# Low part of every fourth down-projection weight piece from a negated ScalarE copy and an accumulating transfer, in a one-core decoder layer

## The chip, the cores and the metric

The kernel runs on one core of a Trainium2 chip. The metric is the device time of one execution in microseconds (us); it is given as the median of several runs.

## What is computed

One decoder layer on 256 tokens of width 2048, in float32. The part that the change touches is the last matrix product, the down-projection of the gated MLP, followed by a residual and a layer norm:

```python
def conv_ffn(x, w_up, conv_w, conv_b, w_down):
    h = x @ w_up                                  # (256, 2048) @ (2048, 11264)
    ...                                           # causal depthwise conv, width 3
    a, b = jnp.split(acc, 2, axis=-1)
    return (jax.nn.silu(a) * b) @ w_down          # (256, 5632) @ (5632, 2048)

x = layer_norm(DN_ALPHA * x + conv_ffn(x, ...), ln2_g, ln2_b)
```

## The kernel before

TensorE multiplies in a float32 format of reduced precision (fp32r). To keep float32 accuracy every operand is split into a high part, which is the value rounded to fp32r, and a low part, which is the value minus the high part; a product is then the sum of three matmuls: high by high, high by low, low by high.

The down-projection is computed in four column blocks of 512 outputs (lines 907 to 917, the last block in a call of its own). Each block is one call of `tok_major`: the weights are the moving operand, the activations `aT` (already split) the stationary one. The 44 contraction tiles of 128 rows are brought in by `pieces` (line 81): one 1 MiB transfer on SP's queue (line 87) loads four tiles into a buffer `raw`, of which there are two (`RAW_BUFS = 2`); the buffer is then split in two pieces of two tiles, 128 x 1024 values each. So a block has 11 raw loads and 22 pieces. For a piece, `split` (line 72) lets ScalarE write the high part `whi` (an `act` copy with rounding, recorded at line 70) and VectorE the low part `wlo` (a subtraction, line 74). `whi` and `wlo` have four buffers each, so a piece's split can begin when TensorE is done with the piece four earlier. TensorE runs 12 matmuls of 512 columns on a piece (lines 149 to 151: per tile and token half one with `whi`, one with `wlo`, one with `whi` again).

A raw buffer is loaded anew when both of its pieces have been split, that is when the last reader of it is done; the loads are issued by SP in order. TensorE's order is written out by hand. The other engines' order in this stage is the scheduler's, with the split of the pieces at high priority in program order. GpSimd (POOL) does nothing for the weights here: at the start of the stage its queue issues two 1 MiB loads of the layer norm's rows (lines 911 and 912), at the end it takes part in the layer norm.

Of the kernel before, what the change touches and what calls it, by code (L numbers as in the profile page):

```python
# [11 lines left out]
AF = mybir.ActivationFunctionType  # L12
ALU = mybir.AluOpType
# [11 lines left out]
KF = DFF // P  # L25
# [16 lines left out]
def hybrid_layer(  # L42
# [6 lines left out]
    nc = tc.nc  # L49
    ctx.enter_context(tc.manual_schedule(engines={ENG.PE}))  # L50
    x2 = x[0]
    win, wup, wout, wdown = w_in[0], w_up[0], w_out[0], w_down[0]

    def hp(level=1):
        return tc.high_priority(offset=1000000 * level)
# [10 lines left out]
    def stt(o, a, s, b, op0, op1):  # L66
        nc.vector.scalar_tensor_tensor(out=o, in0=a, scalar=s, in1=b, op0=op0, op1=op1)  # L67

    def act(o, a, f, **kw):
        nc.scalar.activation(out=o, in_=a, func=f, **kw)  # L70

    def split(hi, lo, src, low=nc.vector):
        act(hi, src, AF.Copy)
        low.tensor_tensor(out=lo, in0=src, in1=hi.bitcast(F32), op=ALU.subtract)  # L74
# [6 lines left out]
    def pieces(w2, col, width, kt_n, big, step, home=None, low=lambda k0: nc.vector):  # L81
        wv = w2.rearrange("(k p) c -> p k c", p=P)
        for b0 in range(0, kt_n, big):
            bn = min(big, kt_n - b0)
            with hp():
                raw = wst.tile([P, bn, width], F32, name="raw", bufs=RAW_BUFS)
                nc.sync.dma_start(out=raw, in_=wv[:, b0:b0 + bn, col:col + width])
            for s0 in range(0, bn, step):
                n = min(step, bn - s0)
                with hp():  # L90
                    hi, lo = (home or stage)(b0 + s0, n, width)
                    split(hi, lo, raw[:, s0:s0 + n, :], low(b0 + s0))
                yield b0 + s0, n, hi, lo

    def stage(k0, n, width):
# [2 lines left out]
    def mm_tile():  # L98
        return ps_mm.tile([P, 2, 512], F32, name="mm")
# [14 lines left out]
    def feat_major(w2, col, xT, kt_n, big=8, step=4, ready=()):  # L114
        ps = mm_tile()
        for piece in ready or pieces(w2, col, 256, kt_n, big, step):
            fm_piece(ps, xT, kt_n, *piece)
        return ps
# [16 lines left out]
                                         stop=kt == kt_n - 1)  # L135
        return ps

    def tok_major(w2, col, xT, kt_n, big=4, step=2, last=0, home=None, done=None, during={}, ends=(512,), mid={}):
        if last:
            ps = [mm_tile()[:, 0, :] for _ in range(NT)]  # L140
        else:
            both = mm_tile()
            ps = [both[:, t, :] for t in range(NT)]

        def go(kt, t, hi, lo, k, o=None, w=slice(0, 512), first=0):
            o = ps[t] if o is None else o
            xs = slice(t * P, (t + 1) * P)
            xl = slice(S + t * P, S + (t + 1) * P)
            nc.tensor.matmul(o[:, w], lhsT=xT(kt)[:, xs], rhs=hi[:, k, w], start=kt == first, stop=False)  # L149
            nc.tensor.matmul(o[:, w], lhsT=xT(kt)[:, xs], rhs=lo[:, k, w], start=False, stop=False)  # L150
            nc.tensor.matmul(o[:, w], lhsT=xT(kt)[:, xl], rhs=hi[:, k, w], start=False, stop=kt == kt_n - 1)  # L151

        kept = []
        for k0, n, hi, lo in pieces(w2, col, 512, kt_n, big, step, home=home):
            if k0 < kt_n - last:
                for k in range(n):
                    for t in range(NT):
                        go(k0 + k, t, hi, lo, k)
                    for f in mid.get(k0 + k, ()):
                        f()  # L160
            else:
                kept.append((k0, n, hi, lo))
                for k in range(n):
                    go(k0 + k, 0, hi, lo, k)
        if last:
            done(0, ps[0], 0, 512)
        c0 = 0
        for c1 in ends if last else ():
            left = last
            o = mm_tile()[:, 0, :] if c0 else ps[1]  # L170
            for k0, n, hi, lo in kept:
                for k in range(n):
                    go(k0 + k, 1, hi, lo, k, o, slice(c0, c1), kept[0][0] if c0 else 0)
                    left -= 1
                    for f in during.get(left, ()):
                        f()
            done(1, o, c0, c1)
            c0 = c1
        return ps
# [47 lines left out]
    def xT(k):  # L227
        return xT_t[:, k, :]
# [72 lines left out]
    pooled = []  # L301

    second = pieces(win, 4096 + 256, 256, KD, 8, 4)
    early = []

# [67 lines left out]
    for j in range(2):  # L373
        ps = tok_major(win, 6144 + 512 * j, xT, KD)
        with hp():
            for t in range(NT):
                act(vg[t][:, 512 * j:512 * (j + 1)], ps[t], AF.Gelu_apprx_tanh)
# [10 lines left out]
    for j in range(4):  # L388
        crow = lv()[0:88, 0:P]
        src = conv_w[0, j] if j < 3 else conv_b[0]  # L390
# [36 lines left out]
    for j in range(4):  # L427
        ps = feat_major(win, 5120 + 256 * j, xT, KD)
# [10 lines left out]
    def hgrn(half):  # L439
        h0 = 4 * half  # L440
        fr, q, v, og = t4(), t4(), t4(), t4()
        for j in range(2):
            ps = feat_major(win, 1024 + 512 * half + 256 * j, xT, KD)
            fm_sum(bc(fr, S)[:, 2 * j:2 * j + 2, :], ps, mix)
        for j in range(2):
            ps = feat_major(win, 512 * half + 256 * j, xT, KD)
            qj = bc(q, S)[:, 2 * j:2 * j + 2, :]
            fm_sum(qj, ps, mix)
            with hp():
                act(qj, qj, AF.Silu)  # L450
        v = v.rearrange("p (t c) -> p t c", t=NT)
        ps = tok_major(win, 2048 + 512 * half, xT, KD)
        with hp():
            for t in range(NT):
                act(v[:, t, :], ps[t], AF.Copy)
        for j in range(2):
            ps = feat_major(win, 3072 + 512 * half + 256 * j, xT, KD)
            oj = bc(og, S)[:, 2 * j:2 * j + 2, :]
            fm_sum(oj, ps, mix)
            with hp():  # L460
                act(oj, oj, AF.Silu)

        return fr, q, v, og
# [153 lines left out]
    def open_gate(gi, j, home, mid={}):  # L617
        ps = tok_major(win, 7168 + D * gi + 512 * j, xT, KD, mid=mid)
        with hp():
            for t in range(NT):  # L620
                act(home[t], ps[t], AF.Sigmoid)
# [125 lines left out]
    for j in range(3):  # L747
        cs = slice(512 * j, 512 * (j + 1))
        ps = tok_major(wout, 512 * j, mT, KD) if j else first_out
# [34 lines left out]
    def wout_during(c):  # L784
        with hp(2):
            ln1_turn(0, c)
            if 0 < c < 3:
                ln1_low(0, c - 1)
            if c == 2:
                pull()  # L790

    tok_major(wout, 1536, mT, KD, last=KEEP, home=keep_home, done=wout_done,
              during={left: [lambda c=c: wout_during(c)] for c, left in enumerate((5, 3, 2, 0))})
# [32 lines left out]
    for j in range(KF // 2):  # L826
        ac = []
        for half in range(2):
            if j == 0 and half == 0:
                ps = ps_first  # L830
            else:
                ps = feat_major(wup, half * DFF + 256 * j, x1T, KD, ready=() if j else chain(up_early, up_next))
# [73 lines left out]

    for j in range(3):
        cs = slice(512 * j, 512 * (j + 1))
        ps = tok_major(wdown, 512 * j, aT, KF)
        if j == 0:  # L910
            nc.gpsimd.dma_start(out=g2[:, 0, :], in_=ln2_g[0].partition_broadcast(P))
            nc.gpsimd.dma_start(out=g2[:, 1, :], in_=ln2_b[0].partition_broadcast(P))
        with hp():
            for t in range(NT):
                stt(x1[:, t, cs], x1[:, t, cs], ALPHA, ps[t], ALU.mult, ALU.add)
                nc.vector.bn_stats(out=st2[:, t, j, :], in_=x1[:, t, cs])
# [43 lines left out]
```

## Time and profile before

| | us |
|---|---|
| median of three runs | 1600.36 |
| their range | 1599.52 to 1601.9 |
| the profiled execution's own time | 1600.03 |
| its span, first to last instruction | 1598.3 |

The profiled execution took 1.7 us more than its span, which lies outside the first and last instruction. Its mean granted TensorE clock was 0.997 of full speed. TensorE is the busiest engine by far; the rows below show how far ahead of it the other engines and the transfers are in the down-projection, which runs from about 1347 us to about 1587 us of the span.

### The profile page before, as it was taken

What the parts mean: (1) busy time and instruction counts of PE and PEld (TensorE: products, weight loads), DVE (VectorE), ACT (ScalarE), POOL (GpSimd) and SP (SyncE); (2) the same over time, 40 slices, a digit from 0 to 9 for tenths busy, and PEclk for the clock granted to TensorE, in tenths of its full rate; (3) what the DMA queues carried; (4) which work ended last, traced back from release to release, by engine and by line L of the source; (5) the groups of instructions that cost most, each with busy time, mean ns of one, the idle gap of its engine ahead of it and who ended that gap; (6) DMA issues with size and microseconds to landing.
All of it is one profiled execution on the core that took longest, in us unless ns stands there. A gap on an engine that the chain in (4) does not pass through costs nothing. (4 is left out here: it accounts for less than half of the span.)

```text
span 1598.3 us, 20294 instructions
## 1 busy us (share of the span) xinstructions
PE 1578.2 (99%) x8129; PEld 1344.8 (84%) x8129; DVE 1001.7 (63%) x1196; ACT 828.8 (52%) x962; POOL 48.4 (3%) x116
## 2 busy tenths in 40 slices
PE   9999999999999999999999999999999999999997
PEld 7888888888888887888888888888888888888886
DVE  6666547765448755447567677676676667445455
ACT  5455558546458555444435555555555555333332
POOL 1100000000000001000003000000000000000001
PEclk9999999999999999999999999999999999999999
DMA  7656555655555547655553655555655556655553
GB/s 246 234 185 198 185 191 174 195 178 169 192 189 172 199 160 263 211 186 183 187 208 106 210 186 184 186 191 194 193 184 185 187 192 231 208 185 201 193 186 130
DMA packets 217213, 305.10 MB, mean 191 GB/s; under 512 B 5148, under 2 KB 137812, under 8 KB 216608
## 3 DMA queue, kind: packets, MB, share of 16 engines
q1 hardware_dynamic: 214912, 294.67, 55.8%
q0 software_dynamic: 2208, 9.16, 1.7%
q8 instruction: 63, 1.03, 0.3%
q14 instruction: 30, 0.25, 0.0%
HBM read 301.71 MB, written 2.10 MB: 190 GB/s over the span
## 5 line engine op out<-in xcount | busy, mean ns | idle before, releaser
L74 DVE TENSOR_TENSOR wlo<-raw,whi 128x1024 fp32r<-128x1024 f32 x541 | 659.1, 1222 | 530.4 <-ACT whi L70 529.7
L70 ACT ACTIVATE whi<-raw 128x1024 fp32r<-128x1024 f32 x543 | 571.1, 1056 | 664.2 <-PE mm L151 281.6
L108 PE MATMUL mm<-x1T,whi 128*128 128x512 f32 x1376 | 432.2, 395 | 0.0
L111 PEld LDWEIGHTS mm<-x1T,wlo 128*128 128x128 f32 x1376 | 258.5, 188 | 61.1
L111 PE MATMUL mm<-x1T,wlo 128*128 128x256 f32 x1376 | 270.3, 278 | 0.0
L150 PE MATMUL mm<-wlo,X 128*128 128x512 f32 x612 | 238.4, 389 | 1.3 <-DVE wlo L74 1.3
L149 PE MATMUL mm<-whi,X 128*128 128x512 f32 x612 | 239.5, 391 | 0.0
L151 PE MATMUL mm<-whi,X 128*128 128x512 f32 x612 | 238.2, 389 | 0.0
L108 PEld LDWEIGHTS mm<-x1T,whi 128*128 128x128 f32 x1376 | 209.4, 189 | 0.0
L108 PE MATMUL mm<-X,whi 128*128 128x512 f32 x640 | 201.5, 396 | 0.9 <-DVE X L74 0.9
L111 PEld LDWEIGHTS mm<-X,wlo 128*128 128x128 f32 x640 | 120.2, 188 | 28.4
L150 PEld LDWEIGHTS mm<-wlo,X 128*128 128x128 f32 x612 | 114.9, 188 | 25.1 <-DVE wlo L74 2.0
L149 PE MATMUL mm<-whi,aT 128*128 128x512 f32 (+1 forms) x352 | 135.2, 384 | 0.0
L150 PE MATMUL mm<-wlo,aT 128*128 128x512 f32 (+1 forms) x352 | 135.2, 384 | 0.0
L151 PE MATMUL mm<-whi,aT 128*128 128x512 f32 (+1 forms) x352 | 135.2, 384 | 0.0
L151 PEld LDWEIGHTS mm<-whi,X 128*128 128x128 f32 x612 | 114.9, 188 | 24.1
L149 PEld LDWEIGHTS mm<-whi,X 128*128 128x128 f32 x612 | 114.9, 188 | 23.5 <-ACT whi L70 0.2
L111 PE MATMUL mm<-X,wlo 128*128 128x256 f32 x640 | 125.8, 278 | 0.0
L108 PEld LDWEIGHTS mm<-X,whi 128*128 128x128 f32 x640 | 97.7, 189 | 1.5 <-DVE X L74 1.2
L150 PEld LDWEIGHTS mm<-wlo,aT 128*128 128x128 f32 x352 | 66.1, 188 | 13.2
L151 PEld LDWEIGHTS mm<-whi,aT 128*128 128x128 f32 x352 | 66.1, 188 | 13.1
L149 PEld LDWEIGHTS mm<-whi,aT 128*128 128x128 f32 x352 | 66.1, 188 | 13.0
(189 smaller groups left out, 1281.1 us busy)
## 6 DMA issues: line engine op xcount, KB each, us to landing
raw<-in_w_in_dram SPq DMA_DIRECT2D x102, 1024.0 KB, 5.0
raw<-in_w_up_dram SPq DMA_DIRECT2D x88, 1024.0 KB, 5.1
raw<-in_w_down_dram SPq DMA_DIRECT2D x44, 1024.0 KB, 5.0
raw<-in_w_out_dram SPq DMA_DIRECT2D x16, 1024.0 KB, 5.1
raw<-in_w_pool_proj_dram SPq DMA_DIRECT2D x8, 1024.0 KB, 5.0
raw<-in_w_sg_proj_dram SPq DMA_DIRECT2D x8, 1024.0 KB, 5.1
raw<-in_w_hg_proj_dram SPq DMA_DIRECT2D x8, 1024.0 KB, 5.0
x<-in_x_dram POOLq DMA_DIRECT2D x4, 512.0 KB, 7.6
```

The source lines that it names most:

```text
L70: nc.scalar.activation(out=o, in_=a, func=f, **kw)
L74: low.tensor_tensor(out=lo, in0=src, in1=hi.bitcast(F32), op=ALU.subtract)
L108: nc.tensor.matmul(ps[:, c, :], lhsT=hi[:, k, c * P:(c + 1) * P], rhs=xT(kt)[:, 0:512], start=kt == 0, stop=False)
L111: nc.tensor.matmul(ps[:, c, 0:256], lhsT=lo[:, k, c * P:(c + 1) * P], rhs=xT(kt)[:, 0:256], start=False, stop=kt == kt_n - 1)
L149: nc.tensor.matmul(o[:, w], lhsT=xT(kt)[:, xs], rhs=hi[:, k, w], start=kt == first, stop=False)
L150: nc.tensor.matmul(o[:, w], lhsT=xT(kt)[:, xs], rhs=lo[:, k, w], start=False, stop=False)
L151: nc.tensor.matmul(o[:, w], lhsT=xT(kt)[:, xl], rhs=hi[:, k, w], start=False, stop=kt == kt_n - 1)
```

## The change

In the first three column blocks of the down-projection, a piece that begins at a contraction tile k0 with k0 % 8 == 2 takes another path. These are the second pieces of every other raw buffer: k0 = 2, 10, 18, 26, 34 and 42, six of the 22 pieces of a block, 18 in all. For such a piece VectorE does nothing. ScalarE writes the high part as before, and then writes the negated, rounded value into the low part's buffer; then an accumulating transfer on GpSimd's queue adds the raw piece, 512 KiB, from SBUF onto that buffer in SBUF. The sum is the raw value minus the high part, as before. All other pieces, the fourth block and every other product of the kernel are left as they are.

```diff
                 with hp():
                     hi, lo = (home or stage)(b0 + s0, n, width)
-                    split(hi, lo, raw[:, s0:s0 + n, :], low(b0 + s0))
+                    src = raw[:, s0:s0 + n, :]
+                    if low(b0 + s0) is None:
+                        act(hi, src, AF.Copy)
+                        act(lo, src, AF.Copy, scale=-1.0)
+                        nc.gpsimd.dma_start(out=lo, in_=src, accum_op=ALU.add)
+                    else:
+                        split(hi, lo, src, low(b0 + s0))
                 yield b0 + s0, n, hi, lo
...
-    def tok_major(w2, col, xT, kt_n, big=4, step=2, last=0, home=None, done=None, during={}, ends=(512,), mid={}):
+    def tok_major(w2, col, xT, kt_n, big=4, step=2, last=0, home=None, done=None, during={}, ends=(512,), mid={},
+                  low=lambda k0: nc.vector):
...
-        for k0, n, hi, lo in pieces(w2, col, 512, kt_n, big, step, home=home):
+        for k0, n, hi, lo in pieces(w2, col, 512, kt_n, big, step, home=home, low=low):
...
     for j in range(3):
         cs = slice(512 * j, 512 * (j + 1))
-        ps = tok_major(wdown, 512 * j, aT, KF)
+        ps = tok_major(wdown, 512 * j, aT, KF, low=lambda k0: None if k0 % 8 == 2 else nc.vector)
```

## Rows read from the trace of the kernel before

**Rows 1.** Busy time by stretch: steady down-projection, then around the first layer norm.

```profile
core 0: us, PE busy (x) PEld busy (x) DVE busy (x) ACT busy (x) POOL busy (x), PEclk, DMA share, GB/s
1365.00:1498.00 133.00, 133.00 (x589) 110.12 (x588) 64.64 (x57) 51.94 (x49) 0.00 (x0) 1.00 0.56 191
...
844.00:847.00 3.00, 1.06 (x7) 0.61 (x6) 3.00 (x3) 0.60 (x1) 3.00 (x2) 1.00 0.00 0
847.00:850.00 3.00, 3.00 (x12) 2.33 (x10) 0.33 (x2) 1.55 (x2) 1.15 (x2) 0.55 0.96 312
...
852.00:858.00 6.00, 5.69 (x51) 5.57 (x50) 5.86 (x7) 2.41 (x4) 2.95 (x3) 1.00 0.29 92
```

**Rows 2.** Waits, 1347 to 1590 us: waiter, releaser, total us, times, longest.

```profile
ACT whi L70 <- PE mm L151: 115.0, 71, 1.7
DVE wlo L74 <- ACT whi L70: 110.2, 76, 3.0
ACT whi L70 <- DMA raw<-in_w_down_dram: 15.5, 7, 3.4
```

**Rows 3.** Timeline of ScalarE: start us, duration, instruction, idle before and releaser.

```profile
1369.15 1.06 ACT L70 ACTIVATE whi<-raw 128x1024 fp32r<-128x1024 f32 x1 [1.66 <-PE mm L151]
1371.87 1.06 ACT L70 ACTIVATE whi<-raw 128x1024 fp32r<-128x1024 f32 x1 [1.66 <-PE mm L151]
1374.59 1.06 ACT L70 ACTIVATE whi<-raw 128x1024 fp32r<-128x1024 f32 x1 [1.66 <-PE mm L151]
1377.31 1.06 ACT L70 ACTIVATE whi<-raw 128x1024 fp32r<-128x1024 f32 x1 [1.66 <-PE mm L151]
```

**Rows 4.** Timeline of VectorE and of SP's queue, same stretch.

```profile
1370.24 1.23 DVE L74 TENSOR_TENSOR wlo<-raw,whi 128x1024 fp32r<-128x1024 f32 x1 [1.49 <-ACT whi L70]
...
1371.50 0.37 SPq L87 DMA_DIRECT2D raw<-in_w_down_dram  x1
...
1376.94 0.37 SPq L87 DMA_DIRECT2D raw<-in_w_down_dram  x1
```

**Rows 5.** Timeline of TensorE, same stretch.

```profile
1376.89 0.39 PE L151 MATMUL mm<-whi,aT 128*128 128x512 f32 x1
1377.11 0.39 PE L149 MATMUL mm<-whi,aT 128*128 128x512 f32 x1
1377.34 0.39 PE L150 MATMUL mm<-wlo,aT 128*128 128x512 f32 x1
```

**Rows 6.** What SP's raw loads waited for, 1343 to 1590 us.

```profile
SPq L87 <- DVE wlo L74: 200.9, 41, 6.3
```

**Rows 7.** Transfer issues of the span: KB each, median us from issue to landing.

```profile
raw<-in_w_down_dram SPq DMA_DIRECT2D x44, 1024.0 KB, 5.0
x<-in_x_dram POOLq DMA_DIRECT2D x4, 512.0 KB, 7.6
gb<-in_ln_b_dram POOLq DMA_DIRECT2D x1, 1024.0 KB, 9.9
x1T<-in_ln_g_dram POOLq DMA_DIRECT2D x1, 1024.0 KB, 5.1
x1T<-in_ln_b_dram POOLq DMA_DIRECT2D x1, 1024.0 KB, 7.4
t<-in_sg_w_dram POOLq DMA_DIRECT2D x1, 512.0 KB, 4.8
t<-in_sg_b_dram POOLq DMA_DIRECT2D x1, 512.0 KB, 4.1
lv<-in_lv_mask_dram POOLq DMA_DIRECT2D x2, 256.0 KB, 3.0
```

**Rows 8.** Transfer queue, 1340 to 1598 us: packets, MB, share of 16 engines.

```profile
q1 hardware_dynamic: 23838, 47.15, 53.7%
```

**Rows 9.** Start of the stage: timelines of POOL and of ScalarE.

```profile
1342.06 0.60 POOL L911 DMA_DIRECT2D x1T<-in_ln_g_dram  x1 [10.23 <-PE mm L111]
1342.65 0.53 POOL L912 DMA_DIRECT2D x1T<-in_ln_b_dram  x1
...
1341.62 1.06 ACT L70 ACTIVATE whi<-raw 128x1024 fp32r<-128x1024 f32 x1 [0.75 <-PE mm L108]
```

## Prediction, made before the changed kernel was run

> **What bounds the kernel now.** I read the table of busy time by stretch first. In the steady part of the down-projection TensorE is busy for the whole 133 us at a granted clock of 1.00, VectorE for 64.6 us and ScalarE for 51.9 us, POOL not at all, and the transfer engines are 56% busy [rows 1]. So TensorE sets the pace, and whatever relieves VectorE relieves an engine that has half its time free: VectorE waits for ScalarE and ScalarE for TensorE, not the other way round, and no wait of TensorE stands in the list of that stretch [rows 2]. No gain is to be had from work taken off VectorE; the question is only whether the new path still delivers in time.
>
> How much time there is, the timelines show. ScalarE starts a high part every 2.72 us (1374.59 less 1371.87), each time when TensorE frees a buffer [rows 3]; that is TensorE's time for one piece of 12 matmuls. With four buffers, the piece whose split starts at 1369.15 is multiplied three pieces after the one that begins behind the freed one: its first matmul is the one at 1377.11, and its low part is needed by the matmul at 1377.34 [rows 3, 5]. The low part is written at 1370.24 + 1.23 = 1371.47 [rows 4]. It is there 5.9 us early.
>
> The second view is of the raw buffers. SP issues the next load 0.03 us behind that low part, at 1371.50 [rows 4]; nearly all of the loads wait for exactly this, the last subtraction on the buffer [rows 6]. The load lands 5.0 us later [rows 7], at 1376.5, and the first high part from it starts at 1377.31 [rows 3]: only 0.8 us of slack. The ring of two raw buffers is tight, while the ring of four split buffers has almost 6 us. This is the point that decides below.
>
> **The change part by part.**
>
> Removed: 18 subtractions on VectorE of 1.23 us [rows 4], 22 us. VectorE is half idle and nothing waits for it but TensorE, 5.9 us later; worth nothing by itself.
>
> Added on ScalarE: 18 negated copies. They have the shape of the high-part copies, so 1.06 us each [rows 3], 19 us in all. Between two high parts ScalarE idles 1.66 us [rows 3], so the next high part isn't moved. The copy does lie on the new chain to the low part, and I count it there.
>
> Added on POOL's queue: 18 accumulating transfers. POOL waits for the copy; behind that wait stand only the next such transfer and perhaps the two loads of the norm's rows [rows 9], which nobody needs until the norm. What matters is the time L from POOL's issue to landing. The trace has no accumulating transfer and none from SBUF to SBUF. The nearest rows: on POOL's queue 256 KB land in 3.0 us, 512 KB in 4.1, 4.8 and, four issued back to back, 7.6 us; 1 MB in 5.1 and 7.4, and at worst 9.9 [rows 7]. The transfer must read 512 KB of raw and 512 KB of the old low part, so it moves more than a 512 KB load. On SP's queue 47.15 MB took 53.7% of the 258 us from 1340 to 1598 [rows 8], 2.94 us per MB, so 3.1 us for 1 MiB and 1.55 for half of it. 4.1 + 1.55 = 5.7; and two 1 MB transfers on POOL's queue, the same bytes read, give 5.1 and 7.4, mean 6.2. I take L = 6.0, between the two, and keep 3.0 and 10 as ends.
>
> The Trainium skill's page "DMA: Bandwidth & Descriptors", section "Anatomy of one DMA — SWDGE (gpsimd) path", gives about 2.0 us plus the bytes at 436 GB/s for a transfer of this queue. By it 512 KiB would be an estimated 3.2 us. The row for 512 KB, 4.1 us, disagrees already for a plain load.
>
> What L does, first to the low part itself. The high part ends 1.06 us after the split begins, the copy 1.06 later, and some 0.1 us go to the hand-over: with L = 6.0 the low part lands 8.2 us after the split's start, and TensorE asks for it 8.2 us after (1377.34 less 1369.15 [rows 3, 5]). One such piece alone would just fit. The price comes from the raw buffer. Its last reader is now the transfer, so the next load into that buffer starts at the transfer's landing, and as SP issues in order, the load of the other buffer stands behind it. All 18 pieces are second halves of every other buffer. Inside a block it is always the same one of the two, so a chain closes upon itself: load 5.0 [rows 7], high part of the first half 1.06, high part of the second half 1.06, negated copy 1.06 [rows 3], hand-overs some 0.25 in all, transfer L, and the next load. Sum 8.43 + L. In that time TensorE has four pieces to do, 4 x 2.72 = 10.88 us. One turn of the chain therefore costs L - 2.45 us of TensorE idle time: 3.55 us at L = 6.0. The four split buffers can't absorb it, since the chain is slower than TensorE in every turn; they lend once per block.
>
> How often. Six such pieces in a block make five turns, 15 in the three blocks (11 loads are odd, so the next block's chain runs in the other buffer and starts anew). The first turn of a chain is partly paid from the lead in the split buffers; carrying the chain along piece by piece, about half of it in the second and third block. In the first block I count it in full: its first such piece is split at 1341.62, and its transfer meets the two 1 MB loads of the norm's rows, issued at 1342.06 and 1342.65 on the same queue [rows 9], which landed in 5.1 and 7.4 us [rows 7]. That makes 13 full turns and two halves, 14 in all.
>
> Sum: 14 x 3.55 = 50 us. The removed and added engine work beside it counts nothing. The profiled execution took 1600.03 us, its span of 1598.3 and 1.7 outside, 0.3 below the median of the runs, 1600.36; so 1600.0 + 50 = **1650 us**. At L = 4.0 it would be 14 x 1.55 = 22, 1622 us; at L = 8.0 14 x 5.55 = 78, 1678 us.
>
> **The rivals.**
>
> *Not slower: the transfer is hidden.* If L is 2.5 us or less, a turn fits into 10.88 us and nothing is lost, 1600 us; up to about 3 the split buffers' lead makes up for the rest. It decides at L of 2.5 to 3. For it: data that never leave SBUF might land sooner than loads. Against it: no load on POOL's queue of half the size or more lands in under 3.0 [rows 7]. Chance 0.08, nearly all of it no change; a gain of more than 0.2% would need TensorE to have waited for VectorE, which the rows don't show, 0.02 of these.
>
> *The second read costs nothing.* Then the plain rows for 256 and 512 KB hold, L from 3.0 to 4.1, at 3.6 14 x 1.15 = 16 us, 1616 us. Chance 0.12. The page named above would lead here too: at 3.2 us it gives 14 x 0.75, about 10 us, 1610.
>
> *The addition is slow or stands in line.* Every word is read, added and written by the transfer engines, which the raw loads hold for 56% [rows 1]. If L is 8 to 10, like the last of several on POOL's queue, 9.9 [rows 7], a turn costs up to 7.55 us and the sum is 78 to 106 us, 1678 to 1706. Chance 0.18. Against the upper end: when the loop is slow, the transfer runs while few loads are under way.
>
> *The clock falls.* Around the first layer norm TensorE was busy for 1.06 us of 3, and in the next 3 us the granted clock was 0.55, near the lower of its two levels (1.2 GHz for 2.4) [rows 1]. Idle stretches of 3.5 us before each late low part could do the same. As long as the clock recovers within the turn it costs nothing: the chain, not TensorE, sets the turn, and the lost time comes out of the idle time. If it stayed low, four pieces would take 21.8 us instead of 10.88, a turn 21.8 instead of 14.43, another 14 x 7.3 = 103 us, 1753. Chance 0.04, as the trace shows TensorE back at 1.00 from 852 to 858 us, once it works on [rows 1]. The Trainium skill's "TensorE: Matmul & The Clock Gate", section "Why this matters for your kernels", advises against idle gaps between bursts of matmuls for this reason; the rows agree that a sparse stretch is followed by a low clock.
>
> **How the numbers follow.** The forecast, L from 4 to 8, has 0.58; with L = 6.0 it is 1650 us, its own range 1622 to 1678. Below it lie 0.20, above it 0.22. The range takes in the cheap transfer down to L of about 3, 1606, and the slow one with L a little over 10 (14 x 7.9 = 110), 1710; outside are the hidden transfer and the fallen clock, and the far tails, under 0.2. About 0.2% (3.2 us) is what a measurement of this kernel can tell from no change. Faster 0.02, same 0.06, slower 0.92.
>
> **What would show it.** In the changed kernel's trace SP's raw loads should wait for the transfer on POOL's queue instead of VectorE's subtraction in every other load; L stands in the list of transfer issues; TensorE should idle at line 150, released by the transfer, some 15 times, 2 to 5 us each, in the first three blocks only, and the fourth block should run as before. If L is 6 and TensorE doesn't idle, the raw chain is wrong; if L is far from 6, only the size of a turn is. If TensorE idles before line 149 instead, released by ScalarE, it is the load or the copy that comes late, not the sum.

## The result

The changed kernel takes 1634.99 us (median), 35 us more than the 1599.94 of the kernel before: the ratio is 1.0217, 95% interval 1.0204 to 1.0231. One of its four executions took 2369.72 us at a mean granted clock of 0.621; it counts in the median and not in the ratio. Slower, as forecast, and by less: 1650 was predicted, with 1606 to 1710 as range. The profiled execution took 1633.91 us, its span is 1632.2.

The wait of the raw loads, 1340 to 1630 us of the changed kernel's span (waiter, releaser, total us, times, longest); [rows 6] shows one line of this kind, VectorE's subtraction:

```profile
SPq L87 <- DMA wlo<-raw: 191.3, 18, 12.8
SPq L87 <- DVE wlo L74: 34.9, 10, 5.0
```

All 18 of the changed pieces now hold a raw load back. The transfer issues of the span (KB each, median us to landing) give L, which answers to [rows 7]:

```profile
raw<-in_w_down_dram SPq DMA_DIRECT2D x44, 1024.0 KB, 5.4
...
wlo<-raw POOLq DMA_DIRECT2D x18, 512.0 KB, 4.5
```

L is 4.5 us where 6.0 was assumed. TensorE, which waited for nothing in this stage before [rows 2], now waits (first TensorE's matmuls, then its weight loads, which show the same waits from another side):

```profile
PE mm L157 <- DMA wlo<-raw: 22.8, 14, 2.5
...
PEld mm L157 <- DMA wlo<-raw: 29.4, 16, 2.9
```

One turn of the chain can be followed instruction by instruction, in the timelines of POOL, SP and ScalarE:

```profile
1385.41 0.84 POOL L96 DMA_DIRECT2D wlo<-raw  x1 [12.20 <-ACT wlo L70]
...
1390.01 0.92 SPq L87 DMA_DIRECT2D raw<-in_w_down_dram  x2
...
1395.24 2.01 ACT L70 ACTIVATE whi<-raw 128x1024 fp32r<-128x1024 f32 x2 [8.23 <-DMA raw<-in_w_down_dram]
1397.16 1.04 ACT L70 ACTIVATE wlo<-raw 128x1024 fp32r<-128x1024 f32 x1
...
1398.49 0.85 POOL L96 DMA_DIRECT2D wlo<-raw  x1 [12.24 <-ACT wlo L70]
```

The transfer issued at 1385.41 lands 4.5 later, at 1389.91; SP issues two loads from 1390.01, the one that waited and the one stuck behind it; ScalarE starts on the data 5.2 us later, makes two high parts and the negated copy, and at 1398.49 the next transfer starts. A turn is 13.08 us, against 10.88 that TensorE needs for four pieces, so each costs 2.2. TensorE's own timeline shows the wait at the place named in the prediction, line 157 (150 before), 1.87 us here:

```profile
1387.66 0.39 PE L156 MATMUL mm<-whi,aT 128*128 128x512 f32 x1
1389.92 0.50 PE L157 MATMUL mm<-wlo,aT 128*128 128x512 f32 x1 [1.87 <-DMA wlo<-raw]
```

Where the time lies, VectorE's evacuations behind the three blocks tell; first the kernel before, then the changed one:

```profile
1407.23 1.28 DVE L67 SCALAR_TENSOR_TENSOR x<-x,mm 128x512 f32<-128x512 f32 x2 [0.40 <-PE mm L151]
...
1467.07 1.29 DVE L67 SCALAR_TENSOR_TENSOR x<-x,mm 128x512 f32<-128x512 f32 x2 [0.40 <-PE mm L151]
...
1526.91 1.29 DVE L67 SCALAR_TENSOR_TENSOR x<-x,mm 128x512 f32<-128x512 f32 x2 [0.40 <-PE mm L151]
```

```profile
1419.00 1.28 DVE L67 SCALAR_TENSOR_TENSOR x<-x,mm 128x512 f32<-128x512 f32 x2 [5.51 <-PE mm L158]
...
1489.31 1.28 DVE L67 SCALAR_TENSOR_TENSOR x<-x,mm 128x512 f32<-128x512 f32 x2 [5.46 <-PE mm L158]
...
1561.06 1.28 DVE L67 SCALAR_TENSOR_TENSOR x<-x,mm 128x512 f32<-128x512 f32 x2 [3.65 <-PE mm L158]
```

From block to block there were 59.84 us; now there are 70.31 and 71.75, 10.5 and 11.9 more. The first block starts with the first matmul on `aT`, here before and after the change, and grew by 12.5:

```profile
1347.16 0.40 PE L149 MATMUL mm<-whi,aT 128*128 128x512 f32 x1
```

```profile
1346.45 0.40 PE L156 MATMUL mm<-whi,aT 128*128 128x512 f32 x1
```

The fourth is as before: from the third evacuation to the end of the span 71.4 us before and 71.1 after.

### The profile page after: what moved, and what is told of

Read it like the earlier page. It is cut to its first block, busy times and chain, and to the rows that moved or that the text cites. A ratio compares the mean times of both kernels' runs of the same rounds, so it can differ in the third digit from the quotient of the medians.

```text
span 1632.2 us, 20369 instructions
## 1 busy us (share of the span) xinstructions
PE 1588.7 (97%) x8129; PEld 1346.3 (82%) x8129; DVE 979.3 (60%) x1178; ACT 841.1 (52%) x980; POOL 63.9 (4%) x134
## 5 line engine op out<-in xcount | busy, mean ns | idle before, releaser
L74 DVE TENSOR_TENSOR wlo<-raw,whi 128x1024 fp32r<-128x1024 f32 x523 | 635.9, 1222 | 573.3 <-ACT whi L70 572.7
L157 PE MATMUL mm<-wlo,aT 128*128 128x512 f32 (+1 forms) x352 | 139.6, 397 | 23.8 <-DMA wlo<-raw 22.8
L156 PE MATMUL mm<-whi,aT 128*128 128x512 f32 (+1 forms) x352 | 137.3, 390 | 0.5 <-ACT whi L70 0.5
L158 PE MATMUL mm<-whi,aT 128*128 128x512 f32 (+1 forms) x352 | 137.0, 389 | 0.0
L156 PEld LDWEIGHTS mm<-whi,aT 128*128 128x128 f32 x352 | 67.1, 191 | 14.6 <-ACT whi L70 0.9
```

## The experiments

The theory (**the chain**): the raw buffer is released by the transfer, and the turn of load, high parts, copy and transfer through one buffer is longer than TensorE's four pieces. The rivals: each transfer's low part is **late by itself**, whatever the buffers do; or the transfers **contend** with the raw loads. Two further questions are what the second read costs, and what the clock does. Each ratio below is to the kernel before, with its 95% interval; the diffs are against the changed kernel, and `...` marks what is left out of them.

**A third raw buffer.** Every third load of a block goes to memory that is free in these three blocks.

```diff
-                raw = wst.tile([P, bn, width], F32, name="raw", bufs=RAW_BUFS)
+                raw = raw_home(b0) if raw_home else None
+                if raw is None:
+                    raw = wst.tile([P, bn, width], F32, name="raw", bufs=RAW_BUFS)
...
+    def third(b0):
+        return extra[:, 0] if b0 // 4 % 3 == 2 else None
...
```

> The changed kernel with a third raw buffer for the first three column blocks, in memory that is free there; all 18 accumulating transfers stay. Chain theory: a buffer then has three loads' time, 6 pieces or 16.3 us of TensorE, for the 13.1 us that a turn takes in the changed kernel, so the loss of 34 us goes: 1600 to 1603 us. Rival 'each transfer is late by itself' (the low part is not there when TensorE asks, some 1.9 us for each of 18 transfers): the low part's own path is unchanged, so 1630 to 1636. Rival 'contention' (the 512 KB transfers slow the raw loads, whose landing rose from 5.0 to 5.4 us): traffic is unchanged, so most of the loss stays, 1620 or more.

Measured: 1612.63 us, ratio 1.0085 (1.0070 to 1.0100). 22 of the 35 us are gone, so the buffer chain carries most of the loss; "late by itself" alone would have left all of it, and the traffic is the same. But 13 us are left, and none were expected. The list of TensorE's waits and the transfer issues of this kernel (`x1T` is the third buffer's name in the trace):

```profile
PE mm L159 <- DMA wlo<-raw: 5.2, 3, 2.6
PE mm L159 <- DMA wlo<-x1T: 3.6, 2, 2.4
```

```profile
wlo<-raw POOLq DMA_DIRECT2D x12, 512.0 KB, 6.2
wlo<-x1T POOLq DMA_DIRECT2D x6, 512.0 KB, 5.9
```

Landing has risen from 4.5 to about 6. The low part may take some 6 us from the end of the copy before TensorE waits (the 8.2 of the prediction less the high part, the copy and the hand-over), so now single transfers are late by themselves: the five waits are all for transfers, and they sum to 8.8 of the 13 us; the rest isn't itemised. The slow transfers run beside raw loads. The extremes of this kernel, as the issues of two short stretches, 1361.0 to 1361.3 us and 1472.7 to 1473.1 us, list them:

```profile
wlo<-x1T POOLq DMA_DIRECT2D x1, 512.0 KB, 4.5
```

```profile
raw<-in_w_down_dram SPq DMA_DIRECT2D x1, 1024.0 KB, 6.6
wlo<-raw POOLq DMA_DIRECT2D x1, 512.0 KB, 9.2
```

The first was issued at 1361.07, into the last 0.24 MB of an earlier load, and SP's next load came only at 1365.73, behind its landing: 4.5 us. The second was issued at 1472.84, a raw load at 1472.87: 9.2 us, and the load took 6.6 instead of 5. With two buffers the chain itself kept the two apart, as each load waited for the transfer to land: 13 of the 18 transfers of the changed kernel ran with no load beside them, and all 13 landed in 4.5 or 4.6 us. With three buffers they meet.

**The control: the third buffer without the new path.**

```diff
-        ps = tok_major(wdown, 512 * j, aT, KF, low=lambda k0: None if k0 % 8 == 2 else nc.vector)
+        ps = tok_major(wdown, 512 * j, aT, KF, raw_home=third)
```

> Control: the kernel before with the third raw buffer alone, no new path. The raw loads are not what sets the time before the change: 1599 to 1601. If this came out lower than the kernel before, the third buffer would bring a gain of its own, and the run with it and the transfers would have to be read against this one.

Measured: 1599.41 us, ratio 1.0002 (0.9992 to 1.0011). The third buffer by itself does nothing.

**The transfer alone taken out.** VectorE adds the raw piece onto the negated copy in its place.

```diff
-                        nc.gpsimd.dma_start(out=lo, in_=src, accum_op=ALU.add)
+                        add(lo, src, lo.bitcast(F32))
```

> The changed kernel with the transfer alone taken out: ScalarE writes the negated copy as before, and VectorE adds the raw piece onto it (1.23 us) in the transfer's place. Chain theory: a turn is about 5.0 + 3 x 1.06 + 1.23 + 0.2 = 9.6 us, under 10.88, so nothing is lost: 1599 to 1601. If the extra ScalarE copies (18 x 1.06 us) cost anything themselves, it shows here: up to 1619.

Measured: 1598.88 us, ratio 0.9998 (0.9989 to 1.0008). ScalarE's 18 extra copies of 1.06 us cost nothing, so the whole loss is the transfer's doing.

**The other half of the buffer.**

```diff
-low=lambda k0: None if k0 % 8 == 2 else nc.vector
+low=lambda k0: None if k0 % 8 == 0 else nc.vector
```

> The changed kernel with k0 % 8 == 0: the same 18 transfers in number, on the first piece of every other buffer instead of the second. Chain theory: the high part of the second half (1.06 us) is no longer ahead of the transfer, so a turn is 13.07 - 1.06 = 12.0 us against 10.88, 1.1 to 1.2 us each, with 15 turns 15 to 18 us: 1615 to 1619. A price for each transfer, or contention: unchanged, 1634.

Measured: 1616.87 us, ratio 1.0111 (1.0096 to 1.0126). The same number of transfers, half the price, because one high part less stands in the turn: this is inside the chain's forecast, and no price for each transfer gives it. That it is the middle of the forecast is in part luck: from transfer to transfer inside the chains POOL's issues lie 10.95 to 13.52 us apart, 12.2 in the mean, and the variant with the copy first, further below, had the same turn forecast and took 8 us longer.

**Every third buffer.**

```diff
-low=lambda k0: None if k0 % 8 == 2 else nc.vector
+low=lambda k0: None if k0 % 12 == 2 else nc.vector
```

> The changed kernel with the new path on pieces with k0 % 12 == 2, every third raw buffer instead of every other: 12 transfers instead of 18, in the two raw buffers by turns. Chain theory: two such pieces in one buffer are 12 pieces apart, so the chain doesn't close on itself and a late load is made up for before the next; only at the two block borders (k0 = 38, then 2) do two fall on neighbouring turns of one buffer, about 2 us each: 1600 to 1606 us. Rivals that price each transfer: 12/18 of 34, 23 us, 1623.

Measured: 1608.37 us, ratio 1.0065 (1.0045 to 1.0085). Far from the 23 us of a price for each transfer, and 2 us beyond the chain's range. What was missed is the same as with the third buffer: the transfers, free of the chain, run beside the loads. This kernel shows it most clearly: behind the first transfer, which meets the loads of the norm's rows, the two that ran while SP's queue moved nothing (issued at 1409.55 and 1472.96) landed in 4.5 us, and the nine beside which it moved 0.6 to 1.0 MB in 4.7 to 8.0. The transfer issues and TensorE's waits:

```profile
wlo<-raw POOLq DMA_DIRECT2D x12, 512.0 KB, 6.3
```

```profile
PE mm L157 <- DMA wlo<-raw: 6.9, 7, 1.7
```

**The copy ahead of the high part.** ScalarE's order is fixed for the two.

```diff
-                        act(hi, src, AF.Copy)
-                        act(lo, src, AF.Copy, scale=-1.0)
+                        with tc.manual_schedule(engines={ENG.Activation}):
+                            act(lo, src, AF.Copy, scale=-1.0)
+                            act(hi, src, AF.Copy)
```

> The changed kernel with ScalarE's two copies of such a piece exchanged: the negated copy first, then the high part; two raw buffers, 18 transfers. Chain theory: the high part (1.06 us) leaves the turn, 13.07 - 1.06 = 12.0 us against 10.88, so 1.1 us a turn, 14 to 15 turns: 1614 to 1618. If the loss were that of the transfer alone, whatever stands ahead of it in the raw buffer's turn, it would stay at 1634.

Measured: 1624.94 us, ratio 1.0160 (1.0143 to 1.0177). The right direction, but 10 us where 17 to 21 were expected. Most turns inside a block are near the forecast of 12.0; POOL's timeline, from a block border on, has 12.19 and 12.16 us from issue to issue in its last three lines:

```profile
1408.87 0.85 POOL L97 DMA_DIRECT2D wlo<-raw  x1 [1.99 <-ACT wlo L70]
1422.00 0.85 POOL L97 DMA_DIRECT2D wlo<-raw  x1 [12.28 <-ACT wlo L70]
1437.20 0.85 POOL L97 DMA_DIRECT2D wlo<-raw  x1 [14.35 <-ACT wlo L70]
1449.39 0.85 POOL L97 DMA_DIRECT2D wlo<-raw  x1 [11.33 <-ACT wlo L70]
1461.55 0.85 POOL L97 DMA_DIRECT2D wlo<-raw  x1 [11.31 <-ACT wlo L70]
```

Two others inside a block, behind transfers of 5.0 and 5.5 us, took 12.67 and 13.12. The turns behind the block borders are longer still: 13.1 and 15.2 us here, with transfers that took 5.0 and 6.4. At a border two such pieces follow each other in different buffers, both loads come late together, and load and transfer meet. That gave the rest back.

**Both: third buffer and copy first.** The edits of the third buffer and, in the same kernel:

```diff
-                        act(hi, src, AF.Copy)
-                        act(lo, src, AF.Copy, scale=-1.0)
+                        with tc.manual_schedule(engines={ENG.Activation}):
+                            act(lo, src, AF.Copy, scale=-1.0)
+                            act(hi, src, AF.Copy)
```

> The third raw buffer and the exchanged copies together. With the third buffer alone 13 us were left, and TensorE waited five times (2.4, 1.7, 1.2, 0.9 and 2.6 us) for transfers that took 6 to 9 us while raw loads were under way. Theory 'the rest is the low part late by itself': with two copies ahead the transfer may take about 6.0 us before TensorE waits, with one 7.1, so each of these waits shrinks by 1.06 us, to some 4 us in all: 1601 to 1606. If the rest were still a chain through a raw buffer, or the traffic itself, 1610 to 1613.

Measured: 1609.91 us, ratio 1.0071 (1.0055 to 1.0087). TensorE's waits:

```profile
PE mm L160 <- DMA wlo<-raw: 4.1, 3, 2.1
PE mm L160 <- DMA wlo<-x1T: 2.5, 2, 1.7
```

Five waits again, 6.6 us where the third buffer alone had 8.8. Four of them stand behind the same transfers as there and shrank by 0.46 to 0.87 us, not by 1.06; the fifth of those, 0.93 us, is gone, and one of 1.15 us is new, behind a transfer that took 8.3 us where it took 6.7 with the third buffer alone. The transfer starts earlier and is still late by itself, since it still meets the loads (median 6.1 us for the two raw buffers). The expected time was missed by 4 us, and the measured one is at the edge of what the rival "the traffic itself" was given, 1610 to 1613: what is left is set by how the transfers meet the loads, more than by the copy ahead of them.

**No addition.** The transfer copies the raw piece over the low part; the down-projection leaves out the subtraction in 18 pieces.

```diff
-                        nc.gpsimd.dma_start(out=lo, in_=src, accum_op=ALU.add)
+                        nc.gpsimd.dma_start(out=lo, in_=src)
```

> The changed kernel with the accumulation taken off the transfer: it copies the raw piece over the low part (the kernel's down-projection then leaves out the subtraction of the high part in 18 pieces). It measures what the addition itself costs. Forecast's view (the second read of 512 KB takes transfer time): landing falls from 4.5 to some 3 to 3.6 us, a turn from 13.07 to 11.6 to 12.2, and 15 turns cost 11 to 19 us: 1611 to 1619. Rival 'the second read is free': landing stays 4.3 to 4.5 and the time 1630 to 1635.

Measured: 1613.82 us, ratio 1.0088 (1.0073 to 1.0103), and the transfer issues say:

```profile
wlo<-raw POOLq DMA_DIRECT2D x18, 512.0 KB, 2.9
```

The addition costs 4.5 - 2.9 = 1.6 us, and a turn is 11.41 us (POOL's issues at 1384.34 and 1395.75). So accumulating isn't free; its price is close to the 1.55 us for half a MiB of the prediction, though the run does not separate the second read from the adding. What was wrong there is the base: the 4.1 us of a 512 KB load from HBM stand against 2.9 from SBUF to SBUF. The turn alone, some 15 x 0.53 = 8 us, does not give the 14.6 us that were measured; the turns behind the block borders, 12.5 to 14.5 us, hold part of the rest. That the time fell into the expected range although the turn was shorter than expected is luck.

**The transfer twice.** Two accumulating transfers in a row, the second waiting for the first; the raw piece is added twice.

```diff
                         nc.gpsimd.dma_start(out=lo, in_=src, accum_op=ALU.add)
+                        nc.gpsimd.dma_start(out=lo, in_=src, accum_op=ALU.add)
```

> The changed kernel with each accumulating transfer issued twice, one waiting for the other (the raw piece is then added twice in 18 pieces). L doubles from 4.5 to 9.0 to 9.3 us. Chain theory: a turn goes from 13.07 to about 17.7 us, 6.8 above TensorE's 10.88, 15 turns: 95 to 105 us, 1695 to 1705, and TensorE idles about 7 us before each late low part. If the clock falls after these idle stretches and this costs time of its own, on top of the chain, the time is longer, up to 15 x 10.9 us more when it stays low through the turns; if the chain absorbs it, 1695 to 1705 holds although the clock is low for part of each turn. Price for each transfer: 34 x 2 = 68 us, 1668.

Measured: 1725.96 us, ratio 1.0793 (1.0777 to 1.0810), 21 us above the chain's range. Part of it is L: the second transfer has a median of 6.0 us, not 4.5, as the other buffer's load has begun meanwhile. The clock is another part. The table of busy time by stretch, in its longest turn (TensorE's busy time stands first, the granted clock third from the end):

```profile
1516.00:1521.00 5.00, 5.00 (x23) 4.14 (x23) 2.39 (x2) 2.12 (x2) 0.61 (x2) 1.00 0.57 108
1521.00:1530.00 9.00, 0.69 (x4) 0.23 (x3) 0.06 (x1) 0.26 (x1) 0.76 (x1) 0.77 0.74 175
1530.00:1537.70 7.70, 7.70 (x22) 6.07 (x23) 1.23 (x1) 2.81 (x3) 0.28 (x1) 0.61 0.41 136
```

```profile
1535.11 1.06 ACT L70 ACTIVATE whi<-raw 128x1024 fp32r<-128x1024 f32 x1 [4.31 <-PE mm L159]
```

TensorE idles 8.3 us, then works at a granted clock of 0.61, and ScalarE's next high part, with its data in place, waits 4.3 us for TensorE to free a split buffer. Matmuls start 0.43 us apart there (1530.55 and 1530.98 in TensorE's timeline), against 0.23 at a granted clock of 1.00, so an estimated half of the 5 us from 1530 to 1535 is the clock's. Behind this idle stretch the low clock did lengthen the turn. How much of the 21 us is the clock's and how much the transfers', this run does not separate.

**Tile by tile.** Copy and transfer in two halves of 512 columns.

```diff
-                        act(lo, src, AF.Copy, scale=-1.0)
-                        nc.gpsimd.dma_start(out=lo, in_=src, accum_op=ALU.add)
+                        for i in range(n):
+                            act(lo[:, i, :], src[:, i, :], AF.Copy, scale=-1.0)
+                            nc.gpsimd.dma_start(out=lo[:, i, :], in_=src[:, i, :], accum_op=ALU.add)
```

> The changed kernel with copy and transfer made tile by tile: negated copy of 512 columns, its 256 KB transfer, then the same for the second tile. Chain theory: the first transfer starts half a copy earlier and each moves half the bytes; from the end of the high part to the second landing some 0.55 x 2 + 0.1 + 3.4 to 3.9 us instead of 5.66: a turn 0.6 to 1.0 us shorter, 1620 to 1627. If two transfers each cost the fixed part of a transfer in line, 1634 or more.

Measured: 1634.82 us, ratio 1.0222 (1.0207 to 1.0237), no better than the changed kernel. The issues of the span, and those of two short stretches (1386.4 to 1386.8 and 1387.6 to 1388.0 us) that hold one half each:

```profile
wlo<-raw POOLq DMA_DIRECT2D x36, 256.0 KB, 4.3
```

```profile
wlo<-raw POOLq DMA_DIRECT2D x1, 256.0 KB, 3.3
```

```profile
wlo<-raw POOLq DMA_DIRECT2D x1, 256.0 KB, 4.3
```

The median of 4.3 mixes two kinds: the first half of the pair issued at 1386.75 lands in 3.3 us, the second, issued 0.86 us behind it, in 4.3. So the pair is done some 5.2 us after its first issue, where one transfer took 4.5, and what the earlier start wins is lost again: POOL's issues at 1386.75 and 1399.69 are 12.94 us apart, against 13.08.

No variant beat the kernel before. That agrees with [rows 1, 2]: TensorE never waited for VectorE, so there was nothing to win.

## Why the prediction was right, and where its sizes were off

**The bound and the sign.** Right. VectorE's 22 us of subtractions were worth nothing, and with the transfer taken out and the extra copies left in, the time was that of the kernel before. (VectorE adds there instead of subtracting, so no run relieves it alone; that its relief is worth nothing rests on [rows 1, 2] and on no variant being faster.)

**The chain.** Right, by its place (line 150, now 157, released by the transfer), its count (14 waits of matmuls, 16 of weight loads, in the first three blocks; some 15 were said), its length and, for 22 of the 35 us, its cure. The waits were shorter than the 2 to 5 us that were said: 22.8 us in 14, 1.6 each, 2.5 the longest. The rest of the 35 us isn't itemised; part of it lies in the stretches of low clock below. The sum 8.43 + L gives 12.93 with the measured L; the trace has 13.08, as a load's data reach ScalarE in 5.2 us, not 5.0.

**L.** This is the term that was mis-sized: 6.0 taken, 4.5 measured, 14 x 1.5 = 21 us too much. The step that failed is the base of 4.1 us, from a load of HBM rows on POOL's queue; a plain transfer from SBUF to SBUF takes 2.9. The 4.1 was a single row, `t<-in_sg_b_dram`, and not a steady one: in the traces of the changed kernel and its variants the same load takes 4.5 to 6.4 us. It is also a broadcast of a short row to all partitions, in another stage of the kernel, so that the memory alone makes the difference isn't shown. The addend of 1.55 for the second read held as a number, 1.6 measured. The two 1 MB rows that raised 5.7 to 6.0 were loads from HBM as well. With L = 4.5 the prediction's own formula gives 14 x 2.05 = 29, 1629 us.

**The number of turns.** 14 were counted, with half a price for the first turn of the second and third block. The growth is 12.5, 10.5 and 11.9 us by block, 34.9 in all, or 16 turns of 2.2. The lead of the split buffers did not pay at the borders: there two transfers follow each other within 3 to 4 us (POOL issues at 1411.58 and 1414.42, 1481.93 and 1485.61) in both buffers, the transfers behind the borders took 5.0 to 5.9 us, and the turns that start with them 13.9 to 14.6. This and the slightly longer turn make the other 6 us, in the other direction than L.

**The first block.** That the first transfer would be slow beside the norm's loads was right: it took 6.1 us, and 15.41 us passed to the next one's issue.

**The clock.** The rival had it falling and costing nothing while it recovers within the turn. It fell three times to 0.50, the lower of its two levels (1.2 GHz). The first, in the table of busy time by stretch and TensorE's timeline of the changed kernel:

```profile
1444.50:1447.00 2.50, 0.25 (x2) 0.00 (x0) 1.17 (x2) 0.00 (x0) 0.00 (x0) 0.95 0.84 159
1447.00:1450.00 3.00, 2.81 (x7) 2.23 (x8) 0.00 (x0) 0.00 (x0) 0.00 (x0) 0.50 0.39 119
1450.00:1453.00 3.00, 3.00 (x15) 2.49 (x14) 0.00 (x0) 0.50 (x1) 0.00 (x0) 0.97 1.06 408
```

```profile
1447.19 0.79 PE L157 MATMUL mm<-wlo,aT 128*128 128x512 f32 x1 [2.44 <-DMA wlo<-raw]
...
1460.27 0.50 PE L157 MATMUL mm<-wlo,aT 128*128 128x512 f32 x1 [0.54 <-DMA wlo<-raw]
...
1473.44 0.50 PE L157 MATMUL mm<-wlo,aT 128*128 128x512 f32 x1 [2.00 <-DMA wlo<-raw]
```

After a wait of 2.44 us the clock is at 0.50 for 3 us; the wait behind it is 0.54 instead of 2.0, and the transfers still follow at 13.1 us. Behind the other two falls the next waits are 0.27 and 0.23 us. The time that the clock took came out of the next wait. That is as argued, for waits of 1.8 to 2.4 us; in the run with the transfer twice, behind a wait of over 8, it was no longer so.

**The other rivals.** The hidden transfer and the free second read both fell: L is above 2.5, and the addition costs 1.6 us. The slow addition fell too, as the longest landing of the changed kernel is 6.1 us; what the prediction said against it, that the transfer runs while few loads are under way, is what the third buffer took away, and there landings of 8.1 to 9.2 us do appear. The estimate of 3.2 us from the Trainium skill's page "DMA: Bandwidth & Descriptors" (section "Anatomy of one DMA — SWDGE (gpsimd) path") is near the plain transfer's 2.9, nearer than the HBM row was; it has no term for an addition.

## What to carry to other kernels

An operation that takes over a buffer's last read has two deadlines: when its result is needed, and when its source must be free. Here the first left some 6 us, enough for a transfer of 4.5; the second had under 1 us to spare before the change and set the time, in a ring of two that returned to the same buffer in every turn. So add up the whole turn of the tightest ring, load to load, and compare it with the bound engine's time for it, before counting what the relieved engine saves; and take a transfer's time from more than one row, with the same two memories and the same neighbours where there are any.

## What was not expected of the hardware

- An accumulating transfer of 512 KB from SBUF to SBUF lands in 4.5 us when no load runs beside it and in up to 9.2 when a 1 MB load is issued at the same time; the load then takes 6.6 instead of 5. The chain that cost the time kept the two apart, and taking the chain away brought them together: 13 of the 35 us stayed.
- A plain transfer of the same size lands in 2.9 us; POOL is busy 0.53 us with its issue and 0.85 with the accumulating one's.
- Two accumulating transfers of 256 KB in a row land in 3.3 and 4.3 us, the second issued 0.86 us behind the first: together no sooner than one of 512 KB.
- Of ten waits of TensorE of 1.8 to 2.5 us in the changed kernel, three (2.44, 2.00 and 1.82) were followed by a granted clock of 0.50, and seven were not: between 1360 and 1400 us, with three waits of 1.9 to 2.5, the mean granted clock is 1.00.
